# A decoder trunk in hi/lo float32r: twelve of thirty-six low weight parts formed by the vector engine instead of by an accumulating transfer

## The chip, the cores and the metric

One core of a Trainium2 chip. The metric is the device time of one execution in microseconds (us); 1099.95 us is the median of three runs of the kernel before.

## The reference, cut to what matters

Two decoder layers over 512 positions with 1024 channels, in float32. Layer 0 mixes by a gated short convolution, layer 1 by windowed attention, both also by attention to 256 memory positions. Each layer ends with a SwiGLU block, and the change lies in that block alone:

```python
for i in range(DEPTH):                      # DEPTH = 2
    ...                                     # mixer: x = x + concat(y_tok, y_mem) @ w_out
    h = rmsnorm(x, norm_ffn[i])
    x = x + (jax.nn.silu(h @ w_gate[i]) * (h @ w_up[i])) @ w_down[i]   # D_FF = 2816
return rmsnorm(x, final_norm)
```

In this text "layer 1" and "layer 2" are the first and the second of them (`i` = 0 and 1).

## The kernel before, in words

**Precision.** A float32 operand is held as two float32r parts: a high part `hi` (a cast on the scalar engine, ACT) and a low part `lo` = value - `hi` (a subtraction on the vector engine, DVE). A product is three matmuls, `hi`·`hi`, `hi`·`lo` and `lo`·`hi` (`mm3`, L129 to L131). So L131 is the matmul that reads the low part of the weights. `split` (L133 to L135) makes both parts: cast on L134, subtraction on L135.

**The SwiGLU block.** The 2816 inner channels are 22 blocks of 128, taken as 11 pairs (256 channels each) in four groups, `SPLITS = ((0, 1), (2, 3, 4), (5, 6, 7), (8, 9, 10))`. Group 0 uses ordinary products. In groups 1 to 3 each pair is made by two units, a gate unit and an up unit, and a unit multiplies its 256 by 1024 weight quarter blocks with the input by a seven-product scheme (Strassen's, in Winograd's form): products 1 to 7, each of 12 matmuls of 128x128 by 128x256 (4 steps of `mm3`). Products 1 and 2 use the weights as they are (`w11`, `w21`), the others use `w22` and four sums, `t1` to `t4`. After each group a down projection (8 results, `p_d`/`d` in the trace) adds the group's part to `x`. Within a group TensorE's order of products is 1, 2, (4 of the unit before), 6, (3 of the unit before), 5, 7, so that product 1 of the up unit follows product 7 of the gate unit, then product 2 of the up unit and product 4 of the gate unit. Products 1, 6, 7 and 4 of a unit add up in one PSUM bank; after 1, 6 and 7 ACT copies the bank out as `r1`, `r6`, `r7` (L733), and the next of them must wait for that copy.

**Names.** `hig_5a`, `log_5a` are the high and low parts of `w11` and `w21` of the gate unit of pair 5, `hiu_5a`, `lou_5a` those of its up unit. `hi..t`, `lo..t` are the parts of the sums. `rawg`, `rawu` are a unit's first loaded half (`w11`, `w21`), `rawbg`, `rawbu` the second (`w22`, `w12`). Buffer numbers and pair numbers of the raw tiles are left out in the trace.

**How a unit's weights are prepared.** Steps with due times relative to the unit's first product, in slots of 1.44 us of TensorE work: `load` (-14), `plain` (-11), `w22` (-6.5), the differences `minus` for `t1`, `t2` (-5.5 and -5, L696), `high(1)`, `low(1)` (-4, -3; L703, L707), the differences that overwrite `w11` and `w21` in the raw buffer (-1.5 and -1, L696), `high(0)`, `low(0)` (0 and 1). `plain` is the step that the change touches: high part by an ACT cast (L685), then `lo` = -`hi` by another ACT instruction (L686), then a transfer issued by GpSimd (POOL, L687) which reads the weights from HBM a second time and adds them onto `lo`.

**Buffers.** The first raw half lies in a ring of two (`raw`), which the down projections' weights share; both parts made by `plain` lie in a ring of four (`wa`), shared with the high parts of the down projections' weights, each freed by the last matmul that reads it. Loads are issued by SyncE (SP) in one queue.

**Order.** The text of the kernel gives only a program order. The framework's scheduler sets the order of each engine at compile time, by program order and by when it reckons that an instruction's inputs and buffers are ready; each engine then runs its own list in order. So an edit may reorder neighbours.

Of the kernel before, what the change touches and what calls it, by code (L numbers as in the profile page):

```python
# [11 lines left out]
FR = mybir.dt.float32r  # L12
# [42 lines left out]
PLAIN = 2  # L55
# [3 lines left out]
def mm_time(n):  # L59

    return n / 2400 + 0.0135


SLOT = 3 * NJ * mm_time(H)
# [11 lines left out]
def yoco_kernel(ctx: ExitStack, tc: tile.TileContext, io: dict):  # L76
# [10 lines left out]
    def wide(name, dt=FR):  # L87

        return slots.tile([P, 2, S], dt, tag="d", name=name, bufs=DBUFS)
# [6 lines left out]
    def pair_of(name):  # L96
        t = wide(name)
        return t[:, 0, :], t[:, 1, :]

    def ps(name):  # L100
        return psum.tile([P, 512], F32, tag="ps", name=name)

    class Queue:


        def __init__(self):
            self.now, self.n, self.items = 0.0, 0, []
# [25 lines left out]
    def split(src, hi, lo):  # L133
        nc.scalar.copy(out=hi, in_=src)  # L134
        nc.vector.tensor_tensor(out=lo, in0=src, in1=hi.bitcast(F32), op=ALU.subtract)  # L135
# [97 lines left out]
    def flat(name, dt, tag):  # L233
        return slots.tile([P, D], dt, tag=tag, name=name, bufs={"raw": 2, "wa": 4, "wt": 4}[tag])
# [309 lines left out]
    first = [ps(f"first{m}") for m in range(6)]  # L544
    for k in range(KD):
        nc.sync.dma_start(out=x[k], in_=io["xT"][k])
        hi, lo = pair_of(f"xa_{k}")
# [114 lines left out]
    class Unit:  # L662


        def __init__(self, src, t0, name, evacuate):
            self.src, self.name, self.evacuate = src, name, evacuate
            self.w, self.bank, self.done, self.r = {}, {}, set(), {}
            W = NJ * P
            d = {}

            def load():
                for c in range(2):
                    d[c] = flat(f"raw{name}", F32, "raw") if c == 0 else wide(f"rawb{name}", F32).rearrange("p a b -> p (a b)")
                    nc.sync.dma_start(out=d[c], in_=src[:, 2 * c * W:2 * (c + 1) * W])
                d["w11"], d["w21"] = d[0][:, :W], d[0][:, W:]
                d["w22"], d["w12"] = d[1][:, :W], d[1][:, W:]

            def halves(hi, lo, names):
                for i, n in enumerate(names):
                    self.w[n] = hi[:, i * W:(i + 1) * W], lo[:, i * W:(i + 1) * W]  # L680

            def plain():

                hi, lo = flat(f"hi{name}a", FR, "wa"), flat(f"lo{name}a", FR, "wa")
                nc.scalar.copy(out=hi, in_=d[0])  # L685
                nc.scalar.activation(lo, hi.bitcast(F32), AF.Copy, scale=-1.0)  # L686
                nc.gpsimd.dma_start(out=lo, in_=src[:, :2 * W], accum_op=ALU.add)  # L687
                halves(hi, lo, ("w11", "w21"))

            def w22():  # L690
                t = wide(f"w22{name}")
                self.w["w22"] = t[:, 0, :], t[:, 1, :]
                split(d["w22"], *self.w["w22"])

            def minus(out, a, b):
                nc.vector.tensor_tensor(out=d[out], in0=d[a], in1=d[b], op=ALU.subtract)  # L696

            def part(n, c):
                return flat(n, FR, "wt") if c else wide(n).rearrange("p a b -> p (a b)")

            def high(c):
                d["hi", c] = part(f"hi{name}t{c}", c)
                nc.scalar.copy(out=d["hi", c], in_=d[c])  # L703

            def low(c, names):
                lo = part(f"lo{name}t{c}", c)
                nc.vector.tensor_tensor(out=lo, in0=d[c], in1=d["hi", c].bitcast(F32), op=ALU.subtract)  # L707
                halves(d["hi", c], lo, names)

            for slot_, fn in (  # L710
                    (-14, load), (-11, plain), (-6.5, w22), (-5.5, lambda: minus("w12", "w12", "w11")),
                    (-5, lambda: minus("w22", "w22", "w12")), (-4, lambda: high(1)),
                    (-3, lambda: low(1, ("t2", "t1"))), (-1.5, lambda: minus("w11", "w22", "w11")),
                    (-1, lambda: minus("w21", "w21", "w22")), (0, lambda: high(0)),
                    (1, lambda: low(0, ("t3", "t4")))):
                work.at(t0 + slot_ * SLOT, fn)
# [24 lines left out]
                self.evacuate(1, 0, self.bank["c"], self.r[6])  # L741
            bg.tick()

    def ffn_units(i, p, t0, h):

        g, u = (slots.tile([P, 2, S], F32, tag="p", name=f"{t}{i}_{p}", bufs=3) for t in "gu")
        gated = set()

        def quarter(t, f, e):
            return t[:, f, e * H:(e + 1) * H]  # L750

        def gate(f, e, bank, r):
            to = quarter(g, f, e)

            def silu(src):
                nc.scalar.activation(to, src, AF.Silu)  # L756
                gated.add((f, e))

            if r is None:
                silu(bank)  # L760
                return
            nc.vector.tensor_tensor(out=to, in0=bank, in1=r, op=ALU.add)  # L762
            work.after(0.9, lambda: silu(to))

        def up(f, e, bank, r):
            work.until(lambda: (f, e) in gated)
            to, by = quarter(u, f, e), quarter(g, f, e)
            if r is not None:
                nc.vector.tensor_tensor(out=to, in0=bank, in1=r, op=ALU.add)
                bank = to  # L770
            nc.vector.tensor_tensor(out=to, in0=bank, in1=by, op=ALU.mult)  # L771
            count[f] += 1
            if count[f] == 2:
                hi, lo = pair_of(f"h{i}_{2 * p + f}")
                work.after(0.8, lambda: nc.scalar.copy(out=hi, in_=u[:, f, :]))  # L775

                def low():
                    nc.vector.tensor_tensor(out=lo, in0=u[:, f, :], in1=hi.bitcast(F32), op=ALU.subtract)  # L778
                    h[2 * p + f] = hi, lo

                work.after(1.6, low)

        count = [0, 0]
        return [Unit(io["w_gate4"][i, p - PLAIN], t0, f"g{i}_{p}", gate),
                Unit(io["w_up4"][i, p - PLAIN], t0 + 7 * SLOT, f"u{i}_{p}", up)]

    def down(h, blocks, name):

# [23 lines left out]
    def ffn(i, xg, norm, g):  # L812


        t, starts, downs = work.now, [], []
# [6 lines left out]
        h, units = {}, {}  # L822
        for s in range(1, len(SPLITS)):
            work.at(downs[s] - 11, weights.open)
            for n, p in enumerate(SPLITS[s]):
                units[p] = ffn_units(i, p, starts[s] + 14 * n * SLOT, h)
        xf = None
        for f in range(2 * PLAIN):
            pg = project(xg, f"g{i}_{f}")
# [6 lines left out]
            u = times_r(pu, norm, f"fu{i}_{f}")  # L836
# [3 lines left out]
            hi, lo = pair_of(f"h{i}_{f}")  # L840
# [21 lines left out]
    nF = Norm("fa")  # L862
    xg = out_proj(ORDER_A, nF, G_FFN0, "oa")
    h = ffn(0, xg, nF, G_FFN0)
    nB = Norm("b")
    raws = mem_load()
# [117 lines left out]
    h = ffn(1, xg, nF, G_FFN1)  # L984
    nE = Norm("e", split_last=True)
    products = down(h, blocks_of(LAST), "d1_")
    for m in range(KD - 2):
        _, acc = next(products)
# [121 lines left out]
```

## Time and profile before

| | |
|---|---|
| median of 3 runs | 1099.95 us (1098.74 to 1100.55) |
| the profiled execution | 1097.84 us, its span 1096.1 us |
| TensorE (PE) busy | 1059.7 us, 97% of the span |
| vector engine (DVE) busy | 752.3 us, 69% |
| scalar engine (ACT) busy | 569.8 us, 52% |
| GpSimd (POOL) busy | 161.0 us, 15% |
[...]
| accumulating transfers (queue q0) | 36 of 512 KB, 18.88 MB, 9.8% of 16 engines' span |
| HBM read | 125.63 MB |

Times in the views are in microseconds from the span's start. [...] An arrow in brackets names what ended the idle time of that engine just before the instruction. In the timelines of TensorE `L129`, `L130` and `L131` are the three matmuls of one `mm3`, and `au`, `bu`, `cu` (`ag`, `bg`, `cg`) the PSUM banks of an up (gate) unit: `au` and `bu` are opened by products 1 and 2.

### The profile page before, as it was taken

To read this page: it belongs to the slowest core of one execution; us is meant where nothing else is said; L and a number is where in the kernel's file an instruction comes from. 1 tells how busy PE (TensorE), PEld (TensorE's weight loads), DVE (VectorE), ACT (ScalarE), POOL (GpSimd) and SP (SyncE) were. 2 spreads that over 40 slices of the span, in tenths; PEclk is the share of its full clock that TensorE was granted. 3 is DMA by queue.
4 is the path that set the end of the run, shared out by engine and by line. 5 is a ranking of instruction groups with operands and counts; after the bars stand their busy time and mean duration, and the time that the engine had idled before them with its cause. 6 is when DMAs were issued, how large, how long until landed. Compare 5 with 4: busy or idle time off the path is not lost.

```text
span 1096.1 us, 16379 instructions
## 1 busy us (share of the span) xinstructions
PE 1059.7 (97%) x6418; PEld 945.0 (86%) x6418; DVE 752.3 (69%) x1219; ACT 569.8 (52%) x1005; POOL 161.0 (15%) x136
## 2 busy tenths in 40 slices
PE   9999999999999899899999999999999999998996
PEld 7787888888998898899788887888799889988986
DVE  7587746797756475665788789658877566566743
ACT  6345625445635453563578578545475355435531
POOL 5321304000000000000222042140010000000002
PEclk9999999999999899899999999999999999999998
DMA  6524133246445534643372321131574464456322
GB/s 202 165 77 131 61 104 100 67 135 185 99 126 157 118 93 147 156 98 109 100 224 85 102 62 59 59 115 49 163 174 101 128 176 100 123 159 140 90 84 77
DMA packets 41829, 128.80 MB, mean 118 GB/s; under 512 B 4716, under 2 KB 8728, under 8 KB 41624
## 3 DMA queue, kind: packets, MB, share of 16 engines
q1 hardware_dynamic: 34432, 104.87, 30.8%
q0 software_dynamic: 5184, 18.88, 9.8%
q10 hardware_dynamic: 2136, 4.01, 1.2%
q8 instruction: 50, 0.82, 0.3%
q14 instruction: 27, 0.22, 0.1%
HBM read 125.63 MB, written 4.47 MB: 119 GB/s over the span
## 4 chain that ended last, share of the span: by engine, by line
PE 33%; DVE 7%; ACT 5%; DMA 4%; issue 2%; POOL 0%; DVEq 0%; ACTq 0%; POOLq 0%
PE au L131 2%; DVE wt L135 2%; ACT ps L948 2%; PE au L129 2%; PE au L130 2%; PE ag L129 1%; PE ag L130 1%; PE ag L131 1%; PE p_d L129 1%; PE d L129 1%; PE p_d L130 1%; PE d L130 1%; PE p_d L131 1%; PE d L131 1%; DMA rawu<-in_w_up 1%
## 5 line engine op out<-in xcount | busy, mean ns | idle before, releaser
L134 ACT CAST wa<-raw 128x1024 fp32r<-128x1024 f32 (+3 forms) x140 | 126.3, 903 | 207.3 <-DMA raw<-in_w_down 68.3
L135 DVE TENSOR_TENSOR wt<-raw,wa 128x1024 fp32r<-128x1024 f32 (+3 forms) x140 | 158.8, 1134 | 73.1 <-ACT wa L134 54.5
L129 PE MATMUL p_d<-h,wa 128*128 128x512 f32 x252 | 98.5, 391 | 2.4 <-ACT wa L134 2.4
L131 PE MATMUL p_d<-h,wt 128*128 128x512 f32 x252 | 98.3, 390 | 0.0
L130 PE MATMUL p_d<-h,wa 128*128 128x512 f32 x252 | 98.1, 389 | 0.0
L129 PEld LDWEIGHTS p_d<-h,wa 128*128 128x128 f32 x252 | 47.3, 188 | 13.6 <-ACT wa L134 4.1
L131 PEld LDWEIGHTS p_d<-h,wt 128*128 128x128 f32 x252 | 47.3, 188 | 10.5 <-DVE wt L135 0.9
L130 PEld LDWEIGHTS p_d<-h,wa 128*128 128x128 f32 x252 | 47.3, 188 | 9.8
L775 ACT CAST h<-u 128x512 fp32r<-128x512 f32 x36 | 22.1, 614 | 46.4 <-DVE u L771 46.4
L129 PE MATMUL d<-h,wa 128*128 128x512 f32 (+1 forms) x112 | 41.2, 369 | 1.6 <-ACT h L775 1.6
L130 PE MATMUL d<-h,wa 128*128 128x512 f32 (+1 forms) x112 | 41.3, 368 | 0.0
L131 PE MATMUL d<-h,wt 128*128 128x512 f32 (+1 forms) x112 | 41.0, 366 | 0.0
L129 PE MATMUL p_cv<-xa,wa 128*128 128x512 f32 x96 | 38.2, 398 | 1.0 <-ACT rb_a L314 1.0
L756 ACT ACTIVATE g<-g 128x256 f32<-128x256 f32 x54 | 22.5, 416 | 30.3 <-DVE g L762 30.2
L778 DVE TENSOR_TENSOR h<-u,h 128x512 fp32r<-128x512 f32 x36 | 24.9, 690 | 18.7 <-ACT h L775 18.2
L130 PE MATMUL p_cv<-xa,wa 128*128 128x512 f32 x96 | 37.4, 390 | 0.0
L131 PE MATMUL p_cv<-xa,wt 128*128 128x512 f32 x96 | 37.4, 390 | 0.0
L696 DVE TENSOR_TENSOR rawbu<-rawbu,rawu 128x512 f32<-128x512 f32 x18 | 12.4, 689 | 25.1 <-DMA rawu<-in_w_up 25.1
L948 ACT ACTIVATE ps<-ps,neg_s 128x256 f32<-128x256 f32 (+1 forms) x48 | 22.6, 471 | 10.9 <-DVE neg_s L945 10.7
L696 DVE TENSOR_TENSOR rawbg<-rawbg,rawg 128x512 f32<-128x512 f32 x18 | 12.4, 691 | 21.4 <-DMA rawg<-in_w_gate 21.2
L856 DVE TENSOR_TENSOR x<-p_d,x 128x512 f32<-128x512 f32 x36 | 24.7, 687 | 2.3 <-PE p_d L131 1.7
L129 PEld LDWEIGHTS d<-h,wa 128*128 128x128 f32 x112 | 21.1, 189 | 5.3 <-ACT h L775 2.1
(1609 smaller groups left out, 3695.7 us busy)
## 6 DMA issues: line engine op xcount, KB each, us to landing
raw<-in_w_down SPq DMA_DIRECT2D x48, 384.0 KB, 3.3
rawg<-in_w_gate SPq DMA_DIRECT2D x18, 512.0 KB, 3.7
rawbg<-in_w_gate SPq DMA_DIRECT2D x18, 512.0 KB, 6.3
rawbu<-in_w_up SPq DMA_DIRECT2D x18, 512.0 KB, 5.7
rawu<-in_w_up SPq DMA_DIRECT2D x18, 512.0 KB, 4.4
raw<-in_a_w_in SPq DMA_DIRECT2D x14, 512.0 KB, 3.5
raw<-in_a_w_out SPq DMA_DIRECT2D x8, 512.0 KB, 3.5
raw<-in_w_gate SPq DMA_DIRECT2D x8, 512.0 KB, 3.5
```

The costliest lines, as they stand in the source:

```text
L129: nc.tensor.matmul(out, lhsT=w[0], rhs=x[0], start=first, stop=False, skip_group_check=reopen)
L130: nc.tensor.matmul(out, lhsT=w[0], rhs=x[1], start=False, stop=False, skip_group_check=reopen)
L131: nc.tensor.matmul(out, lhsT=w[1], rhs=x[0], start=False, stop=last, skip_group_check=reopen)
L134: nc.scalar.copy(out=hi, in_=src)
L135: nc.vector.tensor_tensor(out=lo, in0=src, in1=hi.bitcast(F32), op=ALU.subtract)
L696: nc.vector.tensor_tensor(out=d[out], in0=d[a], in1=d[b], op=ALU.subtract)
L756: nc.scalar.activation(to, src, AF.Silu)
L775: work.after(0.8, lambda: nc.scalar.copy(out=hi, in_=u[:, f, :]))
L778: nc.vector.tensor_tensor(out=lo, in0=u[:, f, :], in1=hi.bitcast(F32), op=ALU.subtract)
L856: nc.vector.tensor_tensor(out=x[m], in0=acc, in1=x[m], op=ALU.add)
L948: nc.scalar.activation(own, own, AF.Exp, bias=neg[:, b:b + 1], accum_out=den[:, b:b + 1])
```

## The change

In the first pair of each of the groups 1 to 3, for the gate unit and the up unit (pairs 2, 5 and 8 in both layers, 12 of 36 units), `plain` calls `split`: the same ACT cast for the high part, and one subtraction of 128x1024 elements on the vector engine, raw half minus high part, for the low part. The ACT instruction of L686 and the transfer of L687 are gone for these units. The registration of the two parts under their names (`halves`) stands earlier in the text, which emits no instruction. The other 24 units are as before.

```diff
--- before.py
+++ after.py
@@ -662,7 +662,7 @@
     class Unit:
 
 
-        def __init__(self, src, t0, name, evacuate):
+        def __init__(self, src, t0, name, evacuate, first):
             self.src, self.name, self.evacuate = src, name, evacuate
             self.w, self.bank, self.done, self.r = {}, {}, set(), {}
             W = NJ * P
@@ -680,12 +680,15 @@
                     self.w[n] = hi[:, i * W:(i + 1) * W], lo[:, i * W:(i + 1) * W]
 
             def plain():
-
                 hi, lo = flat(f"hi{name}a", FR, "wa"), flat(f"lo{name}a", FR, "wa")
+                halves(hi, lo, ("w11", "w21"))
+                if first:
+                    split(d[0], hi, lo)
+                    return
+
                 nc.scalar.copy(out=hi, in_=d[0])
                 nc.scalar.activation(lo, hi.bitcast(F32), AF.Copy, scale=-1.0)
                 nc.gpsimd.dma_start(out=lo, in_=src[:, :2 * W], accum_op=ALU.add)
-                halves(hi, lo, ("w11", "w21"))
 
             def w22():
                 t = wide(f"w22{name}")
@@ -741,7 +744,7 @@
                 self.evacuate(1, 0, self.bank["c"], self.r[6])
             bg.tick()
 
-    def ffn_units(i, p, t0, h):
+    def ffn_units(i, p, t0, h, first):
 
         g, u = (slots.tile([P, 2, S], F32, tag="p", name=f"{t}{i}_{p}", bufs=3) for t in "gu")
         gated = set()
@@ -781,8 +784,8 @@
                 work.after(1.6, low)
 
         count = [0, 0]
-        return [Unit(io["w_gate4"][i, p - PLAIN], t0, f"g{i}_{p}", gate),
-                Unit(io["w_up4"][i, p - PLAIN], t0 + 7 * SLOT, f"u{i}_{p}", up)]
+        return [Unit(io["w_gate4"][i, p - PLAIN], t0, f"g{i}_{p}", gate, first),
+                Unit(io["w_up4"][i, p - PLAIN], t0 + 7 * SLOT, f"u{i}_{p}", up, first)]
 
     def down(h, blocks, name):
 
@@ -823,7 +826,7 @@
         for s in range(1, len(SPLITS)):
             work.at(downs[s] - 11, weights.open)
             for n, p in enumerate(SPLITS[s]):
-                units[p] = ffn_units(i, p, starts[s] + 14 * n * SLOT, h)
+                units[p] = ffn_units(i, p, starts[s] + 14 * n * SLOT, h, n == 0)
         xf = None
         for f in range(2 * PLAIN):
             pg = project(xg, f"g{i}_{f}")
```

## Rows read from the trace of the kernel before

**Rows 1.** The page's first part: busy us (share of the span) and instructions of each engine.

```profile
PE 1059.7 (97%) x6418; PEld 945.0 (86%) x6418; DVE 752.3 (69%) x1219; ACT 569.8 (52%) x1005; POOL 161.0 (15%) x136
```

**Rows 2.** List of waits of TensorE: who waits for what: us, times, longest us.

```profile
PE au L131 <- DMA lou_5a<-in_w_up: 6.6, 2, 4.1
PE au L131 <- DMA lou_8a<-in_w_up: 3.7, 2, 3.1
```

**Rows 3.** TensorE timeline, layer 1, pair 5: start, length, line, operation [idle before <-releaser].

```profile
355.75 0.39 PE L129 MATMUL ag<-xf0s,hig_5t 128*128 128x256 f32 x1
...
361.79 0.58 PE L131 MATMUL au<-xf0x,lou_5a 128*128 128x256 f32 x1 [4.10 <-DMA lou_5a<-in_w_up]
...
368.60 0.28 PE L129 MATMUL au<-xf0s,hiu_5t 128*128 128x256 f32 x1
...
371.47 0.28 PE L129 MATMUL cu<-xf0s,hiu_5t 128*128 128x256 f32 x1
```

**Rows 4.** The same, layer 1, pair 8.

```profile
461.11 0.58 PE L131 MATMUL au<-xf0x,lou_8a 128*128 128x256 f32 x1 [3.09 <-DMA lou_8a<-in_w_up]
...
467.77 0.28 PE L129 MATMUL au<-xf0s,hiu_8t 128*128 128x256 f32 x1
```

**Rows 5.** The same, layer 2, pair 5, then pair 8.

```profile
901.25 0.38 PE L131 MATMUL au<-xf1x,lou_5a 128*128 128x256 f32 x1 [2.48 <-DMA lou_5a<-in_w_up]
...
1000.81 0.39 PE L129 MATMUL ag<-xf1x,hig_8t 128*128 128x256 f32 x1 [1.58 <-ACT r7g L733]
```

**Rows 6.** TensorE by stretch: us, busy (instructions), granted clock, DMA share, GB/s.

```profile
364.00:366.00 2.00, 2.00 (x11) 0.50 0.74 219
...
901.00:903.00 2.00, 1.75 (x14) 1.00 0.80 158
```

**Rows 7.** ScalarE (ACT) timeline: layer 1 pairs 5 and 8, layer 2 pair 5.

```profile
345.70 1.06 ACT L685 CAST hiu_5a<-rawu 128x1024 fp32r<-128x1024 f32 x1 [2.30 <-PE p_d L130]
...
350.75 1.06 ACT L686 ACTIVATE lou_5a<-hiu_5a 128x1024 fp32r<-128x1024 f32 x1
...
355.34 0.36 ACT L733 COPY r6g<-ag 128x256 f32<-128x256 f32 x1
...
359.90 0.36 ACT L733 COPY r7g<-ag 128x256 f32<-128x256 f32 x1
...
450.39 1.06 ACT L686 ACTIVATE lou_8a<-hiu_8a 128x1024 fp32r<-128x1024 f32 x1 [0.16 <-PE p_d L130]
...
460.95 0.37 ACT L733 COPY r7g<-ag 128x256 f32<-128x256 f32 x1
...
901.38 0.37 ACT L733 COPY r7g<-ag 128x256 f32<-128x256 f32 x1
```

**Rows 8.** DMA issues in 336 to 349, then 349 to 362: KB each, us to landing.

```profile
rawu<-in_w_up SPq DMA_DIRECT2D x1, 512.0 KB, 5.1
...
rawg<-in_w_gate SPq DMA_DIRECT2D x1, 512.0 KB, 3.6
rawbu<-in_w_up SPq DMA_DIRECT2D x1, 512.0 KB, 4.4
...
lou_5a<-in_w_up POOLq DMA_DIRECT2D x1, 512.0 KB, 9.6
```

**Rows 9.** VectorE (DVE) timeline, layer 1, pair 5.

```profile
348.56 0.68 DVE L696 TENSOR_TENSOR rawu<-rawu,rawbu 128x512 f32<-128x512 f32 x1
...
350.37 1.23 DVE L707 TENSOR_TENSOR lou_5t<-rawu,hiu_5t 128x1024 fp32r<-128x1024 f32 x1 [0.29 <-ACT hiu_5t L703]
...
354.57 0.42 DVE L762 TENSOR_TENSOR g<-bg,r1g 128x256 f32<-128x256 f32 x1
356.07 0.69 DVE L696 TENSOR_TENSOR rawbu<-rawbu,rawu 128x512 f32<-128x512 f32 x1 [1.08 <-DMA rawu<-in_w_up]
```

**Rows 10.** List of waits of SyncE's DMA queue: us, times, longest us.

```profile
SPq L674 <- DVE lou_5t L707: 10.9, 2, 5.9
```

**Rows 11.** Chain that ended last, 985 to 1003: start, us, what.

```profile
989.68 6.79 DMA rawu<-in_w_up
```

## The prediction, made before the changed kernel ran

> **What bounds the kernel now.** The page first: TensorE is busy 97% of the span [rows 1], so only time in which TensorE stands still or runs slowly can be won, whatever the other engines save. Next the list of what TensorE waited for: its two largest entries are the low parts `lou_5a` and `lou_8a`, the up units of pairs 5 and 8, once in each layer, 10.3 us in all, and they are exactly what the change forms in another way [rows 2]. A wait is not the whole price, so third the TensorE timeline around each. At full pace a matmul starts every 0.12 us (24 from 368.60 to 371.47, 2.87 us) and is shown 0.28 long, so a shown idle time is 0.16 short of what is lost. In layer 1 at pair 5 the wait is 4.10 and ends at 361.79: 4.26 lost, and without it TensorE would have gone on at 357.53. [...] In layer 2 the waits are 2.48 and 0.6, and after the first the clock stays at 1.00 [rows 2, 5, 6]: 2.7 and 0.8 us. The four places cost 7.0 + 5.8 + 2.7 + 0.8 = 16.3 us. Pair 2, the first of group 1, is not in the list.
>
> **The change part by part.** It touches 12 units: gate and up of pairs 2, 5, 8 in two layers.
>
> *Removed:* 12 negated copies on ACT (1.06 us each, 12.7), 12 issues on POOL and 12 transfers of 512 KB. None bounds anything by its busy time; what counts is that `lou_5a` was ready only at the end of a copy at 350.75 + 1.06 and a transfer of 9.6 us [rows 7, 8], near 361.7.
>
> *Added:* 12 subtractions of 128x1024 on the vector engine. The same shape stands in the trace at 1.23 us [rows 9]: 14.8 us of vector engine, 1.23 at a time.
>
> *When the new low part is ready.* It needs the high part (345.70 + 1.06), and a `wa` buffer: the copy of pair 8 is held by a down projection's matmul until 450.39, just as its gate unit begins, and pair 5 is alike [rows 7]. So the subtraction can start near 349.9 and end near 351.2, and TensorE comes to it at 357.53: 6 us to spare. The wait goes at all four places, and the slow clock behind two of them with it.
>
> *What is late next: r7.* Product 4 of the gate unit, 24 matmuls (2.87 us) behind the start of the up unit, adds onto the bank that ACT copies out as r7. In layer 1, pair 5, TensorE would want it at 357.29 (two matmuls ahead of 357.53) + 2.87 = 360.16, and the copy ends at 359.90 + 0.36 = 360.26; TensorE goes on 0.05 later: a wait of 0.15. Pair 8: 460.49 against 461.37, 0.9. Layer 2, pair 5: 901.24 against 901.80, 0.55 [rows 3 to 5, 7]. Layer 2, pair 8: TensorE already waits 1.58 us for r7 after the short `lou` wait [rows 5]; if r7 stays where it is, the 0.8 won is waited out again. With r7 unmoved the gain is (7.0 - 0.15) + (5.8 - 0.9) + (2.7 - 0.55) + 0 = 13.9.
>
> *What moves r7.* In ACT's order it stands behind two high parts of the next gate unit, these behind two differences on the vector engine, and these, in today's order, behind a `rawbu` difference that waits for the load of the next up weights (1.08 us in layer 1, pair 5) [rows 7, 9]. The subtraction moves this load: it reads `raw`, and the differences `w11` and `w21` overwrite `raw` in place. The accumulating transfer read HBM instead, so they could run at 348.56; now they must wait for a subtraction that ends near 351.2. Behind them stand the copy, the `lou_5t` subtraction (350.37 now) and the load of the next up weights; the queue of loads waits for that subtraction [rows 9, 10]. I reckon 351.1 + two differences (1.3) + copy (1.05) + subtraction (1.23) = 354.8 for its issue, 3.2 later than now. But the `rawg` differences don't need this load, and the scheduler orders by readiness, so I expect them ahead of the late `rawbu`. Then the vector engine simply works through: its idle 0.29 + 1.08 = 1.37 us in that stretch takes up the 1.23 that come in, and r7 keeps its place. Against this, two loads with almost no accumulating transfer beside them landed in 3.6 and 4.4 us, one beside such a transfer in 5.1 [rows 8], and the load ahead of the 1.58 us wait took 6.79 [rows 11]: there r7 can come 2.3 earlier. For r7 as a whole the bounds are +2.7 (three places 0 to 0.3 better, the fourth 2.2) and the loss of rival 1; I take +1.0, since only one place has a row that long.
>
> [...]
>
> *What the added work delays: r6.* In the same stretch the silu input `g` (354.57) stands behind a full vector queue, ACT's r6 copy behind it (355.34 + 0.36), and TensorE's product 7 starts at 355.75, 0.05 after it [rows 3, 7, 9]. If the 1.23 us land in front of `g`, TensorE waits up to 1.23 in each of six pairs; what r7 would have cost anyway comes off (0.15, 0.9, 0.55 and all of it at the fourth place), so at most 1.1 + 0.3 + 0.7 + 2 x 1.23 in group 1 = 4.6. If the scheduler lets `g`, ready earlier, pass a weight instruction, it is nothing or a gain of a few tenths. I take 1.0, nearer the low end because the scheduler already orders by readiness, and the weight instructions ahead of `g` are for later products than product 7.
>
> *Gate units.* Their low parts are ready while a down projection runs; the extra 1.23 us delay evacuations of `x` and weights by as much, with the eight PSUM banks as cover: 0, and 0 to 1 us once or twice if a down weight is late. This is inside the 4.6.
>
> **Sum:** 13.9 + 1.0 - 1.0 = 13.9 us; own range of this case 9 to 18 (13.9 - 4.6 up to 16.3 + 1.6, where r7 waits nowhere). The profiled execution took 1097.84 us (span 1096.1) and would take 1083.9. The median of the runs is 2.1 above it, 1099.95: I predict 1086.0, own range 1082 to 1091.
>
> **Rivals.**
> *1. The load chain takes over.* The order stays as it is, `rawg` behind `rawbu`. The late load (issue +3.2; landing 3.6 to 4.4 us later, where it now takes 4.4, from 351.60 to 356.07) puts r7 back by some 2.4 to 3.2 us in pair 5 and 2 to 2.5 in the others: gains of 7.0 - 0.15 - 2.8, 5.8 - 0.9 - 2.2, nothing in layer 2 at pair 5 (0.55 + 2.3 against 2.7), 0.4 at the last place, together 7. At full pace before it, a 3.09 us wait was followed by the low clock, 2.6 us of loss, and a 2.48 us one was not [rows 4 to 6], so up to three such losses may come on top: gain 0 to 8, 1092 to 1100. For it: today's order is this one. Against: the load is no longer the first to be ready.
>
> *2. Slower: the subtraction blocks the vector engine.* Placed directly behind the high part, it would stand at the head from 346.8 to 349.9 waiting for the buffer, and all behind it with it: `g` and r6 come 3.1 + 1.23 = 4.3 us later in six up units, 26 us against the 16.3 won, +10: 1110. It turns the sign from 2.7 us per up unit. [...] Against it: ACT's copy had the same buffer to wait for, and the scheduler did not put it behind its high part (345.70, then 350.75) but where it waited 0.16 us, at pair 8 [rows 7].
>
> *3. The change doesn't do what it says:* the scheduler puts the subtraction behind everything, later than 357.5, and TensorE waits as before: 1100. It would have to stand behind the whole queue that now runs up to the `rawbu` difference at 356.07 [rows 9].
>
> **How the numbers follow.** Forecast 0.70, rival 1 0.21, rival 2 0.06, rival 3 0.03. The range leaves out rivals 2 and 3 and the worse half of rival 1, some 0.19: up to 1095; below, 1081.5, half a microsecond past the best sum. A change of 0.2%, 2.2 us, is about what a measurement of this kernel can tell from none. Rival 1 falls below that in a fifth of its cases (0.04): same 0.07, faster 0.87, slower 0.06.
>
> **What the profile after would show.** No TensorE wait for `lou_5a` or `lou_8a`, and no stretch at clock 0.5 in the two pairs of layer 1. 24 accumulating issues instead of 36. The subtraction starts when the last down projection's matmuls end, with a short wait. The `w11` and `w21` differences stand behind it and the load of the next up weights goes out some 3 us later than now. Rival 1 shows as TensorE waits of 2 us or more on r7 copies, with ACT behind late `rawg` differences; rival 2 as an idle vector engine ahead of the new subtraction. I am wrong if TensorE's waits in the three group starts still sum to 8 us or more in both layers, or if a new wait appears in the attention part, which the change doesn't touch but whose order comes out of the same scheduler.

## The result and the profile after

The changed kernel takes 1086.63 us (median of 4 runs, 1085.42 to 1089.08) where the kernel before took 1099.35 (4 runs on the same chip, 1094.88 to 1100.55): ratio 0.9894, 95% interval 0.9862 to 0.9927. The profiled execution took 1085.42 us with a span of 1083.6, 12.5 us shorter than before, at a mean granted clock of 0.997 (0.990 before).

First the page of the changed kernel, beside [rows 1]: twelve more instructions on the vector engine, as many fewer on ACT and POOL, and TensorE 5.9 us less busy, most of it because no work runs at the low clock in the two pairs any more. Before, the 34 matmuls behind the wait took 6.81 us at pair 5 of layer 1 (361.79 to 368.60 [rows 3], granted clock 0.50 [rows 6]) and 6.66 at its pair 8 (461.11 to 467.77 [rows 4], 0.50 in the stretch 463 to 465), where 34 at full pace (24 from 368.60 to 371.47, 2.87 us [rows 3]) take 4.07: 2.7 and 2.6 us more.

```profile
PE 1053.8 (97%) x6418; PEld 939.8 (87%) x6418; DVE 764.1 (71%) x1231; ACT 556.6 (51%) x993; POOL 150.7 (14%) x124
```

Next TensorE's list of waits (who waits for what: us, times, longest). Both entries of [rows 2] are gone. The first and the third entry below are new or larger: before, `r6u` stood at 0.4 us and `r6g` at 0.7.

```profile
PE au L129 <- ACT r6u L736: 4.2, 4, 1.4
PE p_d L129 <- ACT wa L134: 3.2, 2, 1.6
PE ag L129 <- ACT r6g L736: 2.1, 5, 0.7
```

The TensorE timeline of layer 1, pair 5, answers to [rows 3]: the first matmul that reads `lou_5a` follows its neighbours without an idle time, 0.28 us long.

```profile
358.59 0.28 PE L129 MATMUL au<-xf0x,hiu_5a 128*128 128x256 f32 x1
...
358.83 0.28 PE L131 MATMUL au<-xf0x,lou_5a 128*128 128x256 f32 x1
```

By stretch (us, busy and instructions of TensorE, weight loads, DVE, ACT, POOL, then granted clock, DMA share, GB/s) the clock stays at 1.00 where it stood at 0.50 before [rows 6].

```profile
359.00:361.00 2.00, 2.00 (x19) 2.00 (x19) 1.97 (x5) 0.98 (x4) 0.00 (x0) 1.00 0.93 176
361.00:363.00 2.00, 2.00 (x19) 2.00 (x18) 2.00 (x4) 1.73 (x2) 0.00 (x0) 1.00 1.02 320
```

Where the 12.5 us lie is read from the start of each unit's first matmul in both traces. This table is worked out from those starts: lead of the changed kernel on entering and on leaving each place (the start of the next unit).

| place | lead on entering, us | lead on leaving, us | gained | forecast, without the r6 term |
|---|---|---|---|---|
| start to group 1, layer 1 | 0 | 0.33 | 0.3 | 0 |
| group 1, layer 1 (pair 2) | 0.33 | -1.16 | -1.5 | 0 |
| layer 1, pair 5 | -1.16 | 5.68 | 6.8 | 6.85 |
| layer 1, pair 8 | 5.68 | 9.64 | 4.0 | 4.9 |
| layer 2, group 1 | 9.47 | 9.24 | -0.2 | 0 |
| layer 2, pair 5 | 9.24 | 9.37 | 0.1 | 2.15 |
| layer 2, pair 8 | 9.37 | 12.31 | 2.9 | 0 (to 2.2) |

The largest win and the sum are near what was forecast. Four places are not: the last gave more, and at the three that gave less TensorE waits for `r6u`, 1.40 us at pair 2 of layer 1, 0.93 at its pair 8 and 1.43 at pair 5 of layer 2 (the last two also for `r6g`, 0.50 and 0.73). The next rows show how such a wait comes about, at pair 2 of layer 1. First SyncE's queue (the load of pair 3's up weights), then ACT, then TensorE:

```profile
263.87 0.33 SPq L674 DMA_DIRECT2D rawu<-in_w_up  x1
```

```profile
266.74 1.05 ACT L706 CAST hig_3t<-rawg 128x1024 fp32r<-128x1024 f32 x1 [0.28 <-DVE rawg L699]
270.84 1.05 ACT L689 CAST hiu_3a<-rawu 128x1024 fp32r<-128x1024 f32 x1 [3.05 <-DMA rawu<-in_w_up]
271.79 0.38 ACT L759 ACTIVATE g<-ag 128x256 f32<-128x256 f32 x1
272.06 1.05 ACT L690 ACTIVATE lou_3a<-hiu_3a 128x1024 fp32r<-128x1024 f32 x1
273.01 0.36 ACT L736 COPY r6u<-au 128x256 f32<-128x256 f32 x1
```

```profile
273.43 0.39 PE L129 MATMUL au<-xf0s,hiu_2t 128*128 128x256 f32 x1 [1.40 <-ACT r6u L736]
```

ACT stood 3.05 us at the head of its queue, waiting for the load; the copy that TensorE needed was three instructions behind, though the last matmul of the product that it copies had started at 268.87. And why the load is late is in the vector engine's timeline of layer 1, pair 5, beside [rows 9]:

```profile
350.85 0.69 DVE L699 TENSOR_TENSOR rawbg<-rawbg,rawg 128x512 f32<-128x512 f32 x1 [1.54 <-DMA rawg<-in_w_gate]
351.46 1.22 DVE L135 TENSOR_TENSOR lou_5a<-rawu,hiu_5a 128x1024 fp32r<-128x1024 f32 x1
...
354.33 0.69 DVE L699 TENSOR_TENSOR rawu<-rawbu,rawu 128x512 f32<-128x512 f32 x1
354.93 0.42 DVE L765 TENSOR_TENSOR g<-bg,r1g 128x256 f32<-128x256 f32 x1
355.27 0.68 DVE L699 TENSOR_TENSOR rawu<-rawu,rawbu 128x512 f32<-128x512 f32 x1
357.99 1.23 DVE L710 TENSOR_TENSOR lou_5t<-rawu,hiu_5t 128x1024 fp32r<-128x1024 f32 x1 [2.04 <-ACT hiu_5t L706]
```

```profile
359.24 0.33 SPq L674 DMA_DIRECT2D rawu<-in_w_up  x1
```

The chain goes: new subtraction, the two differences that overwrite `raw`, ACT's copy, the `lou_5t` subtraction, and at once the load (359.22 and 359.24). Before, that load went out at 351.62; with TensorE 1.2 us later in this pair, it is 6.4 us later against the matmuls. Nor does the chain run without gaps: two other instructions of the vector engine stand between the subtraction and the first difference, and ACT's copy starts about 1 us after the second one ends. At pair 5 of layer 1 the load still lands in time (5.0 us); at pair 2 it took 6.9. In all six group starts the load goes out 0.64 or 0.65 us behind the up unit's first matmul. Where TensorE waits for `r6u` it lands after 6.4 to 6.9 us; in the other three places ACT can cast after 4.9 to 5.0. What makes it land late in three of the six isn't settled: the transfer of the next gate unit (`log_3a`, `log_6a`, `log_9a`) goes out 2.2 to 2.5 us ahead of it in all six.

### The profile page after: what moved, and what is told of

Its sections match the earlier page's. It is cut to its first block, busy times and chain, and to the rows that moved or that the text cites. A ratio compares the mean times of both kernels' runs of the same rounds, so it can differ in the third digit from the quotient of the medians.

```text
span 1083.6 us, 16325 instructions
## 1 busy us (share of the span) xinstructions
PE 1053.8 (97%) x6418; PEld 939.8 (87%) x6418; DVE 764.1 (71%) x1231; ACT 556.6 (51%) x993; POOL 150.7 (14%) x124
## 3 DMA queue, kind: packets, MB, share of 16 engines
q0 software_dynamic: 3456, 12.58, 6.8%
## 4 chain that ended last, share of the span: by engine, by line
PE 37%; DVE 7%; ACT 4%; DMA 3%; issue 1%; POOL 0%; DVEq 0%; ACTq 0%; POOLq 0%
PE p_d L129 2%; PE p_d L130 2%; PE p_d L131 2%; ACT ps L951 2%; PE au L129 2%; PE au L130 2%; PE au L131 2%; PE ag L129 1%; PE ag L131 1%; PE ag L130 1%; PE d L129 1%; PE d L130 1%; PE d L131 1%; DMA rawg<-in_w_gate 1%; DVE wt L135 1%
## 5 line engine op out<-in xcount | busy, mean ns | idle before, releaser
L135 DVE TENSOR_TENSOR w22g<-rawbg,w22g 128x512 fp32r<-128x512 f32 x18 | 12.3, 686 | 19.0 <-ACT w22g L134 19.0
L129 PEld LDWEIGHTS d<-h,wa 128*128 128x128 f32 x112 | 21.1, 189 | 5.2 <-ACT h L778 1.9
L130 PEld LDWEIGHTS d<-h,wa 128*128 128x128 f32 x112 | 21.2, 189 | 3.8 <-DVE h L135 0.4
```

The source lines that it names most:

```text
L129: nc.tensor.matmul(out, lhsT=w[0], rhs=x[0], start=first, stop=False, skip_group_check=reopen)
L130: nc.tensor.matmul(out, lhsT=w[0], rhs=x[1], start=False, stop=False, skip_group_check=reopen)
```

## The experiments

Two theories stood at the start. Theory 1: the wait was that for the up unit's accumulating transfer, so the up units' half of the change brings all of the gain, and the gate units' half nothing. Its rival: the gain is that of the traffic taken off the DMA engines. Theory 2: what the change gives back comes through the late load above. All ratios are against the kernel before on the same chip, with 95% intervals.

**One half alone.** The up units only:

```diff
-        return [Unit(io["w_gate4"][i, p - PLAIN], t0, f"g{i}_{p}", gate, first),
+        return [Unit(io["w_gate4"][i, p - PLAIN], t0, f"g{i}_{p}", gate, False),
```

> Only the six up units form their low part on the vector engine; the six gate units keep copy and accumulating transfer. Theory 1 (the gain is the four waits for the low parts of up units and the slow clock behind two of them): all of the gain stays, 1086.6 plus or minus 2, no wait for lou_5a or lou_8a. Rival (the gain is the traffic that 12 transfers no longer bring): half of the 12.7 us, some 1093. Theory 2 (what the change gives back comes through the late load of the next up weights, behind the subtraction of the up unit): TensorE waits for r6u copies stay, 0 to 1.4 us at each group start.

Measured: 1084.65 us, ratio 0.9892 (0.9864 to 0.9921), the whole gain. `lou_5a` and `lou_8a` are gone from TensorE's list, and `r6u` stands in it with 4.4 us, as theory 2 has it. Then the gate units only:

```diff
-                Unit(io["w_up4"][i, p - PLAIN], t0 + 7 * SLOT, f"u{i}_{p}", up, first)]
+                Unit(io["w_up4"][i, p - PLAIN], t0 + 7 * SLOT, f"u{i}_{p}", up, False)]
```

> Only the six gate units form their low part on the vector engine; the up units keep copy and accumulating transfer. Theory 1: the four waits for lou_5a and lou_8a stay as in the kernel before, 1099 plus or minus 2.5, with the low clock behind the two longest. Rival (traffic): half of the gain, some 1093. The load of the up weights of the same pair goes out 3 to 5 us later than before, under a down projection, with no wait of TensorE from it.

Measured: 1088.5 us, ratio 0.9915 (0.9883 to 0.9946). Theory 1 is refuted by this in its second half: the accumulating transfers of `lou_5a` and `lou_8a` are all there, and TensorE's list of waits has neither of them. Issues of the kernel before at pair 5 first (SyncE's queue, then GpSimd's), then the transfer view of this run for the stretch 350 to 362 (KB, us to landing) and its SyncE queue show what changed:

```profile
351.62 0.33 SPq L674 DMA_DIRECT2D rawu<-in_w_up  x1
352.00 0.42 SPq L674 DMA_DIRECT2D rawbg<-in_w_gate  x1
```

```profile
352.10 0.87 POOL L687 DMA_DIRECT2D lou_5a<-in_w_up  x1 [12.28 <-ACT r1g L733]
```

```profile
lou_5a<-in_w_up POOLq DMA_DIRECT2D x1, 512.0 KB, 5.9
```

```profile
356.31 0.33 SPq L674 DMA_DIRECT2D rawu<-in_w_up  x1
356.69 0.43 SPq L674 DMA_DIRECT2D rawbg<-in_w_gate  x1
```

The same transfer, issued here at 353.26, lands after 5.9 us in place of 9.6 [rows 8], and the two loads that went out 0.48 and 0.10 us ahead of it now go out 3.05 and 3.43 behind it. The gate unit's subtraction also reads a raw buffer, and holds the chain of loads back by 4.7 us (351.62 to 356.31).

**Groups 2 and 3 only**, since group 1 had no wait to win and lost 1.5 us:

```diff
-                units[p] = ffn_units(i, p, starts[s] + 14 * n * SLOT, h, n == 0)
+                units[p] = ffn_units(i, p, starts[s] + 14 * n * SLOT, h, n == 0 and s > 1)
```

> Group 1 (pair 2, four units) is left as in the kernel before; pairs 5 and 8 as in the changed kernel. In the traces group 1 lost 1.3 us in layer 1 and 0.2 in layer 2 by the change, through the wait of 1.4 us for an r6 copy. Theory 2: this comes back, 1085.2, between 1083.5 and 1086.6, with group 1 within 0.3 us of the kernel before and no r6u wait at pair 2. Rival (traffic): four of twelve transfers come back and with them a third of the gain, 1091.

Measured: 1086.67 us, ratio 0.9908 (0.9878 to 0.9939). In layer 1 the 1.5 us of group 1 do come back (pair 3 starts 0.3 us after its start in the kernel before), but the lead at the end is 12.5 us against 12.3: what is won there is lost elsewhere before layer 2 (lead on entering 8.4 against 9.5). The trace shows where: TensorE waits 0.98 and 1.19 us for `r6g` at pairs 5 and 8 of layer 1 (0.18 and 0.50 in the changed kernel), and behind a wait of 2.2 us for `h` (1.5 there) the granted clock is 0.63 and 0.52 in the stretches 521 to 523 and 523 to 525. Why these waits are longer isn't settled, and the expected gain isn't there.

**Traffic put back**, first kernel: in each changed unit GpSimd copies one column of the new low part into a spare tile and then adds two quarter blocks of 256 KB onto it, the second waiting for the first. Nothing reads the tile, so the result is that of the changed kernel; 28 shared slots in place of 29 pay for it (no run has 28 slots alone). The lines that make the spare tile are left out here:

```diff
                     split(d[0], hi, lo)
+                    nc.gpsimd.tensor_copy(out=dummy[:, 0:1], in_=lo[:, 0:1].bitcast(F32))
+                    for c in range(2):
+                        nc.gpsimd.dma_start(out=dummy, in_=src[:, c * W:(c + 1) * W], accum_op=ALU.add)
                     return
```

> The changed kernel, and for each of the 12 units the removed traffic is put back without anyone waiting for it: once the low part is formed, GpSimd issues two accumulating transfers of 256 KB each onto a tile that nobody reads (the ring of 4 KB buffers has 28 instead of 29 places to make room, which by itself changes no engine's order). Theory 1: the four waits stay away, and most of the gain with them. The transfers run beside the loads of the next weights, so r6u waits may grow by up to 2 us at each of six group starts: 1086 to 1095, likeliest 1089. Rival (traffic is the gain): back to 1098 or more.

Measured: 1119.5 us, ratio 1.0209 (1.017 to 1.0248), far over what theory 1 allows. GpSimd's timeline and SyncE's queue in layer 1, pair 5, then ACT:

```profile
364.19 0.87 POOL L691 DMA_DIRECT2D dummy<-in_w_up  x1 [3.49 <-DMA dummy<-in_w_up]
364.73 1.23 POOL L696 DMA_DIRECT2D log_6a<-in_w_gate  x1
```

```profile
365.84 0.33 SPq L676 DMA_DIRECT2D rawu<-in_w_up  x1
```

```profile
374.22 1.05 ACT L694 CAST hiu_6a<-rawu 128x1024 fp32r<-128x1024 f32 x1 [4.46 <-DMA rawu<-in_w_up]
```

The chained second part is issued 1.65 us ahead of the critical load, with `log_6a` right behind it, and the load takes 8.4 us (365.84 to 374.22) where it took 5.0. TensorE's waits for `r6u` grow from 4.2 to 15.4 us and those for `r6g` from 2.1 to 10.1, and some of its work runs at the low clock again (0.50 in the stretch 915 to 918, for one). So was it the traffic, or its place? The second kernel issues one transfer of 512 KB per changed unit as soon as the high part is there, at pair 5 of layer 1 8.4 us ahead of the up unit's first matmul (5.2 in the kernel before):

```diff
                     split(d[0], hi, lo)
+                    nc.gpsimd.tensor_copy(out=dummy[:, 0:1], in_=hi[:, 0:1].bitcast(F32))
+                    nc.gpsimd.dma_start(out=dummy, in_=src[:, :2 * W], accum_op=ALU.add)
                     return
```

> The changed kernel plus one accumulating transfer of 512 KB in each first unit, issued by GpSimd after the high part as in the kernel before, onto a tile that nothing reads (a sum that no one uses; the result is that of the changed kernel). Unlike the two chained ones of the first traffic kernel it never waits for another of its kind inside a unit. If that kernel's loss of 33 us over the changed one came from GpSimd's queue (two chained transfers of 3.5 us each, with the low part of the next pair behind them), this one costs 1 to 6 us: ratio 0.990 to 0.996. If it came from the traffic as such, 12 us or more: ratio over 1.000.

Measured: 1085.52 us, ratio 0.9883 (0.986 to 0.9907): the same bytes cost nothing there. At pair 5 that transfer is issued 9 us ahead of the load (GpSimd's timeline, then SyncE's queue):

```profile
349.61 0.86 POOL L690 DMA_DIRECT2D dummy<-in_w_up  x1 [0.30 <-POOL dummy L689]
```

```profile
358.66 0.33 SPq L676 DMA_DIRECT2D rawu<-in_w_up  x1
```

The traffic as such is not what was won. That its place decides, ahead of or beside a load that someone waits for, is the likely reading; the two kernels also differ in the size and number of the transfers and in GpSimd's queue, which wasn't taken apart.

**Is company what made the transfer late?** Theory A: the transfer took 9.6 us because two loads went out with it. Theory B: it takes that long anyway, and the gate-only kernel helped in another way. In the kernel before, the loads alone are moved: the load of the second pair's up weights must follow a one-column copy out of the first pair's low part. The lines that keep the low parts in `lows` are left out here:

```diff
                 for c in range(2):
                     ...
+                    if c == 0 and name[0] == "u" and int(name.split("_")[1]) % 3 == 0:
+                        before = lows[name.replace("3", "2").replace("6", "5").replace("9", "8")]
+                        nc.sync.dma_start(out=d[0][:, 0:1], in_=before[:, 0:1].bitcast(F32))
                     nc.sync.dma_start(out=d[c], in_=src[:, 2 * c * W:2 * (c + 1) * W])
```

> The kernel before, all its accumulating transfers kept; only the loads of the second pair's up weights in each group are held back until the first pair's low part lou_2a, lou_5a or lou_8a has landed (a one-column copy out of the low part goes into the raw tile ahead of its load, and is overwritten by it). In the kernel before two of these loads (issued at 351.62 and 352.00) ran beside lou_5a (issued 352.10, landed after 9.6 us); in the gate-only kernel they were issued at 356.31 and lou_5a landed after 5.9 us. Theory A, company (the transfer is late because the loads run beside it): lou_5a and lou_8a land after 6 to 7.5 us, TensorE's waits for them fall from 4.2 and 3.0 us to under 2, and 6 to 11 us are saved: ratio 0.990 to 0.995 of the kernel before. Theory B, the transfer itself (8.5 us or more whatever runs beside it, so that only taking it out helps): the waits stay, the loads are late on top of it, ratio 1.000 to 1.004.

Measured: 1102.43 us, ratio 1.0034 (1.0014 to 1.0055). On the transfer theory A holds: `lou_5a` and `lou_8a` land after 5.4 to 5.8 us in all four places, and TensorE waits for neither. On the time it doesn't: the loads now go out so late (369.54 in place of 351.62 at pair 5) that the wait moves to the copies. From the transfer view, SyncE's queue and TensorE's list:

```profile
lou_5a<-in_w_up POOLq DMA_DIRECT2D x1, 512.0 KB, 5.4
```

```profile
369.54 0.33 SPq L679 DMA_DIRECT2D rawu<-in_w_up  x1
```

```profile
PE au L129 <- ACT r6u L739: 14.9, 7, 2.8
```

The lead shows both sides: 4.8 and 2.9 us are won at pairs 5 and 8 of layer 1, and 5.5 are lost in group 1 of layer 1, where there was no wait to win.

**Starting the transfer earlier.** In the kernel before the copy into `lou_5a` starts 4.0 us after its source is ready, with the `wa` buffer as the likely reason [rows 7]. With a fifth buffer (and 28 shared slots, as in the kernels below with a third raw buffer):

```diff
-            bufs={"raw": 2, "wa": 4, "wt": 4}[tag]
+            bufs={"raw": 2, "wa": 5, "wt": 4}[tag]
```

> The kernel before with five wa buffers in place of four (28 shared slots). In the kernel before the scaled copy into lou_5a started at 350.75, 4 us after its source hiu_5a was ready (345.70 plus 1.06), when its buffer had been released. If that start is half of the old wait, a fifth buffer lets the copy and so the transfer begin up to 4 us earlier, and even at 9 us the transfer lands before TensorE asks (357.6): the waits for lou_5a and lou_8a fall from 10.3 us to under 4: ratio 0.987 to 0.993 of the kernel before. If the scalar queue and not the buffer sets the start, the waits stay: ratio 0.997 to 1.001.

Measured: 1086.25 us, ratio 0.9896 (0.9861 to 0.9931), as good as the change. The transfers still have company and land after 8.9 to 9.2 us, but they start earlier (at pair 5 of layer 1 the copy 9.5 us ahead of the up unit's first matmul in place of 6.5): TensorE's waits for both low parts are 1.4 us in all.

```profile
PE au L131 <- DMA lou_8a<-in_w_up: 0.8, 2, 0.5
PE au L131 <- DMA lou_5a<-in_w_up: 0.6, 1, 0.6
```

**A third raw buffer** (28 shared slots) takes away what makes the loads wait. In the kernel before, and then in the changed kernel:

```diff
-            bufs={"raw": 2, "wa": 4, "wt": 4}[tag]
+            bufs={"raw": 3, "wa": 4, "wt": 4}[tag]
```

> The kernel before with three raw buffers in place of two (and 28 in place of 29 shared slots to pay for them, which by itself changes no instruction). The load of the next up weights then needn't wait for the buffer of the pair in front, and goes out some 5 us earlier, ahead of the low part's transfer. Theory A (company): the transfers have less beside them, TensorE's waits for lou_5a and lou_8a (10.3 us of wait in all) lose half or more: ratio 0.990 to 0.996. Theory B (the transfer itself): the waits stay, ratio 0.998 to 1.001.

Measured: 1086.67 us, ratio 0.9879 (0.9851 to 0.9906). The time is below what theory A gave (0.990 to 0.996), and its reason isn't there: the loads beside the transfer are other ones, but they still go out 0.1 to 0.75 us ahead of it, it lands after 8.0 to 8.8 us, and 8.4 of the 10.3 us of waits stay.

```profile
PE au L131 <- DMA lou_5a<-in_w_up: 4.3, 2, 2.5
PE au L131 <- DMA lou_8a<-in_w_up: 4.1, 2, 2.0
```

The gain is spread over the group starts (3.6 us by pair 3 of layer 1, 2.3 and 3.0 at its pairs 5 and 8, 2.3 in layer 2's group 1; 2.7 are lost again between its pairs 5 and 8, most of it in a wait of 2.4 for a down weight's low part). At pairs 5 and 8 of layer 1 two things show: the waits are shorter (2.5 and 2.0 us where they were 4.1 and 3.1), and there is less low clock behind them: it is back at 1.00 in the stretch 363 to 365 at pair 5, and stays there from 456 to 464 at pair 8. The gains in the two groups 1 were not followed further. In the changed kernel:

> The changed kernel with three raw buffers in place of two (28 shared slots). If the new 4.2 us of waits for the copy r6u come from the load that the subtraction holds back through the raw buffer, the load no longer stands behind the subtraction: r6u waits under 1 us in all, 1083 us, or ratio 0.985 to 0.989 of the kernel before. If they come from the transfer log_6a, which runs beside the load whenever it is issued, the waits stay over 3 us: ratio 0.989 to 0.991.

Measured: 1069.8 us (1069.45 to 1070.74), ratio 0.9736 (0.9711 to 0.9761), 16.8 us below the changed kernel and the fastest of all, far below the 1083 us expected. The load of pair 6's up weights goes out at 339.65 (359.24 with two buffers), ACT's cast of it follows its neighbours without a wait, and `r6u`, `r6g` and the low parts are all gone from TensorE's list:

```profile
339.65 0.33 SPq L674 DMA_DIRECT2D rawu<-in_w_up  x1
```

```profile
354.35 1.05 ACT L706 CAST hig_6t<-rawbg 128x1024 fp32r<-128x1024 f32 x1
355.31 1.04 ACT L689 CAST hiu_6a<-rawu 128x1024 fp32r<-128x1024 f32 x1
```

By the leads against the changed kernel, 7.9 of 16.0 us are won inside the groups, where the waits for `r6u` and `r6g` were 6.3, and 8.1 ahead of group 1 (4.24 in layer 1, 3.81 from its last pair to layer 2's first); the waits for `p_d`'s weights fall from 3.2 to 0.5. The third buffer also changes the order of the instructions on ACT and the vector engine; how much of the gain is order and how much the buffer itself wasn't separated.

**Each half with three buffers**, to complete the table, and the subtraction in all 36 units:

> The changed kernel with the subtraction in the up units alone, and three raw buffers. With both kinds of unit changed and three buffers the time was 1069.8 us. If the gate units' part adds nothing (as with two buffers, where up units alone gave 1084.65 us and both gave 1086.63), 1068 to 1073 us, without waits for lou_5a and lou_8a and with under 2 us of waits for r6u. If the gate units' part counts once the raw buffer no longer binds, 1075 us or more.

> The changed kernel with the subtraction in the gate units alone, and three raw buffers. Company theory: with two buffers the gate units' part helped because it moved the loads of the second pair from 351.62 to 356.31, out of the way of lou_5a's transfer. With three buffers two loads go out beside that transfer (in the kernel before with three buffers at 347.66 and 348.04, the transfer at 348.15, landing 8.4 us), so TensorE's waits for lou_5a and lou_8a come back, 6 to 9 us in all: 1078 to 1088 us. Rival, that the gate units' subtraction helps the up unit in another way, whatever the loads do (an earlier copy, a freer ScalarE): those waits are under 2 us, 1068 to 1074 us.

> Three raw buffers, and the subtraction in all 36 units in place of the first two of each group. It adds 24 subtractions of 1.23 us to VectorE (29.5 us on 759 busy) and takes 24 copies of 1.06 us from ScalarE and the last 24 accumulating transfers from GpSimd. With three buffers TensorE waits for no transfer any more, so if what is left is TensorE's own work, the time stays: 1067 to 1072 us. If VectorE is too full for it, TensorE's waits for the copies r6 or r7 come back by 5 us or more: 1075 us or more. If transfers of the later units still cost something that no wait shows, under 1066 us.

| subtraction in the first pair's | two raw buffers: us, ratio | three raw buffers: us, ratio |
|---|---|---|
| neither (kernel before) | 1099.35 | 1086.67, 0.9879 |
| gate units | 1088.5, 0.9915 | 1072.51, 0.9776 (0.9743 to 0.9809) |
| up units | 1084.65, 0.9892 | 1070.86, 0.9763 (0.9726 to 0.98) |
| both (the change) | 1086.63, 0.9894 | 1069.8, 0.9736 (0.9711 to 0.9761) |
| all 36 units | not run | 1069.91, 0.9751 (0.9719 to 0.9783) |

Up units alone came out as expected. Gate units alone didn't: I expected company and 1078 to 1088 us, and the waits for `lou_5a` and `lou_8a` are 0.2 us. The rival's number is right, but not its reason: the transfer has no company at its start here either. It goes out at 347.17, and the loads follow 2.15 us later:

```profile
349.32 0.33 SPq L674 DMA_DIRECT2D rawg<-in_w_gate  x1
349.70 0.45 SPq L674 DMA_DIRECT2D rawbg<-in_w_gate  x1
```

```profile
lou_5a<-in_w_up POOLq DMA_DIRECT2D x1, 512.0 KB, 5.7
```

With the subtraction everywhere the vector engine takes 28.2 us more, q0 is empty, 12.58 MB fewer are read, and the time stays: TensorE is 98% busy and the list has no weight transfer left to win.

## Why the prediction was right

**The bound and the price of the wait.** Right. The four waits and the two stretches at low clock were the thing to win, and pair 5 of layer 1 gave 6.8 us for a forecast 6.85. The terms 7.0 and 5.8 of the sum are a wait and the low clock behind it, read from the trace before: 4.10 + 0.16 us of standing still and 2.7 of low clock at pair 5 of layer 1, 3.09 + 0.16 and 2.6 at its pair 8. At pair 5 it came back.

**When the new low part is ready.** Right in effect, sized 1.6 us early: I had the subtraction from 349.9, held by a `wa` buffer; it started at 351.46, held by no buffer but behind a difference that itself waited 1.54 us for a load. TensorE came to it at 358.83, with 6 us to spare as forecast.

**r7.** Too dark. I took 2.4 us off and put 1.0 back. In the changed kernel TensorE waits for no `r7` at all, and the 1.58 us of [rows 5] are gone. The `rawg` differences do stand ahead of the late `rawbu` one, as I expected (360.78 and 361.39 against 364.25), and the scheduler also moved the copy ahead of the two high parts that it stood behind:

```profile
358.79 0.37 ACT L736 COPY r7g<-ag 128x256 f32<-128x256 f32 x1 [0.31 <-PE ag L131]
...
360.78 1.05 ACT L706 CAST hig_6t<-rawbg 128x1024 fp32r<-128x1024 f32 x1
```

These are ACT's rows at pair 5 of layer 1, beside [rows 7]. That is why rival 1 did not come. At pair 8 of layer 2 the order is the same (`r7g` at 985.91, the two high parts at 987.90 and 989.23), and that is why it gave 2.9 where I had put 0.

**r6.** The term that was mis-sized: 1.0 forecast, with 4.6 as its bound; the waits for `r6u` and `r6g` are 6.3 us where they were 1.1, so 5.2 are lost, past the bound. I looked for it in the gate units, where 1.23 us of subtraction could land in front of `g`. Most of it is in the up units, by a chain that I had half written down: the later load. I put its issue 3.2 us later and followed it to the vector engine only; at pair 5 of layer 1 it went out 6.4 later, and its other reader is ACT's cast of the next high part, with the `r6u` copy queued behind it. The two errors, about 3 us too dark on `r7` (2.4 less 1.0, and 1.7 of the old wait) and 4 too bright on `r6`, nearly cancel in the sum of 13.9, and the span came out 12.5 shorter. So the price of the waits was understood, but that the total came so near, 1086.63 us for 1086.0, is in part luck. (Two sums of the prediction are out by under 0.1 and change nothing: 2.48 + 0.16 is 2.64, not 2.7, and the terms of 354.8 add up to 354.7.)

**Gate units at 0.** Right as a part of the whole change (up units alone are as fast as both), wrong as a statement on the edit by itself: alone it saves 0.85%, because it moves loads. I had taken the transfer's 9.6 us as its length. The trace of before had the counter-example in it: `lou_2a`, the same transfer in group 1, where I only noted that it wasn't in the list of waits, lands after 5.7 and 5.5 us, with the loads 2.5 and 2.8 us behind it.

**Rival 2** did not come: the subtraction waited for no buffer at the head of the queue. **Rival 3** neither: 24 accumulating issues are left, and all four waits are gone. The signs of being wrong stayed away too: TensorE's waits in the three group starts sum to 4.6 us in layer 1 and 4.4 in layer 2 (`p_d`, `r6g` and `r6u`; the limit was 8), and its list has no new entry in the attention part.

## What to carry to other kernels

A wait for a transfer has three ways out: do the work on an engine (here 1.06%), start the transfer earlier (1.04%), or keep its neighbours away. The third depends on the means: by the gate units' subtraction it gave 0.85%, by holding the loads back it lost 0.3%, since the loads were then late themselves. Before pricing it, look at the same transfer at all its places: a length that changes from 5.7 to 9.6 us points to its company. And when an edit makes an engine read a buffer that a transfer left alone, follow the next load of that buffer to every reader of it, on every queue; here a third buffer, which frees this load (and also changes the order of instructions), was worth more than the change itself.

## What the runs showed of the hardware

In these traces an accumulating transfer of 512 KB is late when loads go out just ahead of it or with it. All rows are `lou_5a` and `lou_8a`, four each, except the last, and are worked out from the timelines of GpSimd and SyncE and the transfer views:

| kernel | next two loads against the transfer's issue | landing, us |
|---|---|---|
| before | first from -0.48 to +0.70 us | 9.6, 8.7, 9.3, 7.3 |
| before, three raw buffers | first from -0.75 to -0.49 | 8.8, 8.0, 8.4, 8.4 |
| before, five wa buffers | first from +0.03 to +0.07 | 9.2, 8.9, 9.2, 9.1 |
| gate units, three raw buffers | first at +2.15 | 5.7, 5.9, 5.8, 5.5 |
| gate units | first at +3.05 to +4.22 | 5.9, 5.9, 5.9, 5.5 |
| before, loads held back | none until it has landed | 5.4, 5.8, 5.8, 5.7 |
| before, `lou_2a` (two places) | first at +2.51, +2.82 | 5.7, 5.5 |

The next pair's accumulating transfer goes out 2.9 to 6.2 us behind in all these rows, late and punctual alike, so it isn't what sets them apart. Of all 340 accumulating transfers in the traces of eleven kernels (all but the two with the spare tile), 98 have a SyncE transfer issued within 1.2 us of them: they land after 6.5 to 10.6 us, median 8.1. Those 119 that have such transfers only from 1.8 to 4 us behind them land after 5.3 to 7.7, median 5.8, and the 83 without any within 4 us after 5.4 to 7.7, median 5.7. So each of the 98 with company at its start took 6.5 us or more, while some without it took up to 7.7; why isn't settled. One exception stands outside the count: with one transfer onto the spare tile, two of its twelve landed after 5.9 and 6.0 us with a load for a down projection 0.3 us ahead of them.

Two loads issued 2.15 us behind a transfer that still has 3.6 us to go cost it nothing that shows: with the subtraction in the gate units and three raw buffers it lands after 5.5 to 5.9 us, against 5.4 to 5.8 with no load at all. It is the loads that take longer: the second of the two lands after 7.8 to 9.5 us in these four places, where three loads in [rows 8] took 3.6 to 5.1. That is measured for transfers of this size alone.

The length of a wait alone doesn't tell whether the low clock follows it. In the kernel before, 2.48 us of waiting was followed by a granted clock of 1.00 [rows 5, 6]; with three raw buffers 2.46 us was followed by 0.50 in the stretch 359 to 361, and with groups 2 and 3 only, 2.19 us by 0.52 in the stretch 523 to 525.

The last surprise is the spread. The changed kernel with three buffers ran from 1069.45 to 1070.74 us (4 runs; 6 runs with the subtraction everywhere: 1069.3 to 1070.64), at a mean granted clock of 0.996 to 0.998, and the kernel before on one chip from 1093.62 to 1105.28 (17 runs), at 0.986 to 0.993, its longest run at the lowest clock. That the missing waits for weights make the difference isn't shown: the list of up units alone with three buffers has no wait for a weight transfer either, and it ran from 1068.89 to 1073.26.
